# A hybrid decoder block on one core: the q, k, v and attention-gate projections as seven products of halves, later tokens first

## The chip, the core and the metric

The kernel runs on one core of a Trainium2 chip. The core has five engines, each with its own instruction queue that is worked through in order: TensorE (PE, matrix products, which go to PSUM), VectorE (DVE), ScalarE (ACT), GpSimd (POOL) and SyncE (SP), which here only issues DMAs. SBUF is the working memory, 128 partitions wide; PSUM has eight banks of 128 x 512 float32, of which this kernel gives two each to the names `z`, `s`, `o` and `t`. The metric is the device time of one execution in microseconds, the median of several runs.

## What is computed

One decoder layer over 2048 tokens of width 1024, cut to what matters here:

```python
h = rms_norm(x, norm_w) * (1 + scale) + shift          # scale, shift from c
z = h @ w_in                                           # 1024 -> 10240
a, b, g_conv, q, k, v, g_attn, m_conv, m_attn = split(z)
u = silu(layer_norm(causal_conv(a * sigmoid(b)))) * silu(g_conv)
q, k = rope(rms_norm(q, q_norm_w)), rope(rms_norm(k, k_norm_w))   # 12 heads of 128
for group (window, dilation) in ((128, 1), (512, 4), (2048, 16)): # 4 heads each
    o_g, lse_g = dilated_window_attention(q, k, v)
o = sum over groups of softmax(lse) * o_g              # 512 wide
y = sigmoid(m_conv) * (u @ w_conv_out) + sigmoid(m_attn) * ((o * silu(g_attn)) @ w_attn_out)
out = x + gate * (y @ w_out)
```

The attention works on blocks of 128 queries. A block of the group with dilation 16 sees only its own keys; the other groups' blocks also see the block before them of the same residue class, if there is one.

## The kernel before

Every float32 operand of a projection is split into a high part (rounded to the format `float32r` by a ScalarE copy) and a low part (the difference, a subtraction on VectorE or GpSimd, with both of its inputs in SBUF). A product is three matmul terms for each 128 rows of the contraction: high by high, high by low, low by high.

The stages in order:

1. **Start.** The conditioning, the rotary tables (`tab`), the loads of x.
2. **q, k, v.** Twelve heads, one "unit" `u` each, in the order of `GROUPS`; in a unit 16 token blocks `j`. `project_step` runs 24 matmuls (`z_tokens`, L369): the stationary operand is 128 tokens of h, the moving one 384 weight columns (q, k and v of the head). Then it takes sums of squares on ScalarE, a reciprocal root on GpSimd (`rsqrt_cols`, L112 and L113), and the rotary turn on VectorE (L397 to L407), with one SBUF tile as output. During unit 0 the kernel also makes h itself (`h_part`) and writes it to memory (`h_d`).
3. **Attention beside it.** For the first eight units (dilations 4 and 16) q, k, v go to memory (`qkv_d`, L760) and are gathered again by stride (`strided`). The last four units are attended from SBUF. `attend_step` is four parts (`turn_qk`, `scores`, `turn_p`, `values`), one part per block step, entered between the matmuls by `hooks`. `values` writes one DMA per block (L469): 128 output columns with the two softmax numbers behind them.
4. **Gate and merge.** For each of two halves of the 512 gate columns, 16 blocks of 24 matmuls of 256 columns (`merge_z`, `pzg`); `merge_step` weighs the three groups' outputs, multiplies by the gate and writes the result transposed to `ai_d`.
5. **The other columns of w_in** (a, b, g_conv, m_conv, m_attn). They are already done as seven products of halves: tokens and contraction are halved, `column_steps` forms the weight combinations T1 to T4 on GpSimd and splits them, `quad` runs the seven products (L954), the token combinations S1 to S4 lie in `s_d`. The convolution runs on VectorE beside it (`conv_parts`, L1003 to L1043).
6. **Three output projections.**

TensorE's order is the program's own from `pe_order` on (`manual_schedule`). The other engines' order is made by a planner from a timeline that it simulates; inside a queue nothing overtakes. `reuse_waits="tile"` on a pool means that a new tile waits for the last use of the tile whose place it takes.

The lines the argument touches: `z_tokens` (L362), `project_step` (L378), `attend_step` (L419), `merge_load` to `merge_step` (L474 to L528), `unit_weights` (L533), the loop over units (L724), the merge loop (L843), and `column_steps` and `quad` (L896, L944) as the pattern of the new code.

Of the kernel before, what the change touches and what calls it, by code (L numbers as in the profile page):

```python
# [18 lines left out]
P = 128  # L19
# [3 lines left out]
NB = S // P  # L23
TAPS = 31
# [11 lines left out]
GROUPS = (1, 2, 0)  # L36
# [18 lines left out]
def tile_hybrid_block(  # L55
# [22 lines left out]
    qkv_d = {u: dram.tile([S, 3, P], F32, name=f"qkv{u}_d") for u in range(2 * NH)}  # L78
    acc_d = [dram.tile([S, NG, ACC_W], F32, name=f"acc{h}_d") for h in range(NH)]
# [10 lines left out]
    s_d = dram.tile([2, 4, 4, P, 512], F32, name="s_d")  # L90

    t_d = {}
# [22 lines left out]
    tabs_c = pool("tabs")  # L115
    tabs = tabs_c.__enter__()

    tab = tabs.tile([P, NB, 2, 64], F32, tag="tab", name="tab0")
    with pool("start", side="right") as st:
        keep = tc.keep_in_program_order  # L120
# [90 lines left out]
        keep(nc.vector.tensor_scalar(a, a, -2.0, 1.0, op0=ALU.mult, op1=ALU.add))  # L211
        last_mm = {k: ada_row(k) for k in (0, 2, 4, None, 6, 7)}
# [10 lines left out]
    hpool_c = [tc.tile_pool(name=f"hT{i}", bufs=1, side="right", reuse_waits="tile") for i in range(2)]  # L223
    hpools = [c.__enter__() for c in hpool_c]

    def quarter_tile(kh, t, hl, name, dtype=F32R):

        return hpools[0 if t == 0 or (kh, t) == (0, 2) else 1].tile([P, 4, 512], dtype, tag=f"h{hl}{kh}{t}", name=name)

    hi, lo = ({(kh, t): quarter_tile(kh, t, hl, f"hT_{hl}_{kh}{t}") for kh in range(2) for t in range(4)} for hl in ("hi", "lo"))  # L230

    def part(x, k, t0, w, nk=1):

        q = x[k // 4, t0 // 512]
        ks = k % 4 if nk == 1 else slice(k % 4, k % 4 + nk)
        return q[:, ks, t0 % 512 : t0 % 512 + w]


    wpool_c = tc.tile_pool(name="wp0", bufs=8, side="right", reuse_waits="tile")
    wp = wpool_c.__enter__()  # L240
    xpool_c = tc.tile_pool(name="xp", bufs=6, side="right", reuse_waits="tile")
    xp = xpool_c.__enter__()
    hx = {}

    def load_x(j, eng=nc.sync):

        xt = xp.tile([P, D], F32, tag="x", name=f"x{j}")
        i0 = eng.dma_start(xt, x2[P * j : P * j + P, :])
        if j >= 4:
            tc.keep_in_program_order(i0)  # L250
        junk = xp.tile([P, 512], BF16, tag="xn", name=f"xn{j}", bufs=1)
        st = xp.tile([P, 4], F32, tag="st", name=f"xst{j}")
        hx[j] = xt
        halves = [slice(0, 512), slice(512, 1024)]

        def square(i):
            ins = nc.scalar.activation(junk, xt[:, halves[i]], AF.Square, scale=1.0 / 32.0,
                                       accum_out=st[:, i : i + 1])
            if i == 1:
                nc.gpsimd.tensor_add(st[:, 0:1], st[:, 0:1], st[:, 1:2])  # L260
                rsqrt_cols(st[:, 1:2], st[:, 0:1], 1, st[:, 2:3])
            return ins

        def scale(i):
            return nc.scalar.activation(xt[:, halves[i]], xt[:, halves[i]], AF.Copy, scale=st[:, 1:2])

        return [lambda: square(0), lambda: square(1), lambda: scale(0), lambda: scale(1)]

    def h_turn(j, kk, tag="t"):

        pt = bank(tag, f"pt_x{j}_{kk}")
        for a in range(2):
            k = 2 * kk + a
            for b in range(2):
                nc.tensor.transpose(pt[:, 256 * a + P * b : 256 * a + P * b + P], hx[j + b][:, P * k : P * k + P], ident)
        return pt

    def h_first(kk, pt):
        for a in range(2):
            k = 2 * kk + a  # L280
            last = nc.scalar.activation(part(hi, k, 0, 256), pt[:, 256 * a : 256 * a + 256], AF.Identity,
                                 scale=mod[:, KC + k : KC + k + 1], bias=mod[:, k : k + 1])
        for a in range(2):
            k = 2 * kk + a
            hf = xp.tile([P, 2, 256], F32, tag="hf", name=f"hf0_{k}", bufs=2)
            nc.vector.tensor_scalar(hf[:, 0], pt[:, 256 * a : 256 * a + 256], mod[:, KC + k : KC + k + 1],
                                    mod[:, k : k + 1], op0=ALU.mult, op1=ALU.add)
            (nc.gpsimd if a else nc.vector).tensor_tensor(part(lo, k, 0, 256), hf[:, 0], part(hi, k, 0, 256).bitcast(F32),  # L288
                                                          op=ALU.subtract)
            nc.sync.dma_start(h_d[k, :, :256], hf[:, 0])  # L290
        return last

    def h_part(j, kk):
        pt = h_turn(j, kk)
        hf = xp.tile([P, 2, 256], F32, tag="hf", name=f"hf{j}_{kk}", bufs=2)
        for a in range(2):
            k = 2 * kk + a
            nc.vector.tensor_scalar(hf[:, a], pt[:, 256 * a : 256 * a + 256], mod[:, KC + k : KC + k + 1],
                                    mod[:, k : k + 1], op0=ALU.mult, op1=ALU.add)
# [1150 lines left out]
```

## Time and profile before

| | |
|---|---|
| three runs | 2433.52, 2436.54, 2439.67 us (median 2436.54) |
| profiled execution | span 2433.6 us from the first to the last instruction; the page gives no other time of it |
| mean granted TensorE clock | 0.994 |
| stages by the trace | q, k, v and attention from about 45 to 1108 us, gate and merge to 1203 |
| DMA | 372.99 MB, mean 153 GB/s |

The profile's page gives the busy time of each engine (PE matmuls, PEld weight loads), then busy shares in 40 slices, the DMA queues, the chain of work that ended last, and the costliest groups of instructions. In a group's line stand source line, engine, operation, output and inputs by tile names, shapes, count, then busy time and mean duration, then the idle time before the group and what ended it. Durations of pipelined instructions overlap, so the distance between two starts is the price of one. Answers about one source line give the shortest, median and longest duration in ns.

### The profile page before, as it was taken

Reading aid. Unit: us, or ns where it says so; the run is one execution under the profiler, and the core shown is the slowest. Engines: PE = TensorE matmul, PEld = TensorE weight load, DVE = VectorE, ACT = ScalarE, POOL = GpSimd, SP = SyncE. Lnnn points to the kernel's source line nnn. Section 1 sums busy time; section 2 is a strip of 40 time slices with the busy share of each in tenths; the row PEclk is TensorE's granted clock in tenths of the full one; section 3 lists DMA queues with packets and bytes.
Section 4 is the critical chain, followed back from the end, with each engine's and each line's share of the span. In section 5 each row is a group of like instructions: output and inputs, shape, how many; then the busy total and the mean of one; then the engine's idle time right before and its main releaser. Section 6 shows DMA issues by size and latency. Waiting matters only on the chain.

```text
span 2433.6 us, 39444 instructions
## 1 busy us (share of the span) xinstructions
PE 2395.2 (98%) x12881; PEld 2138.5 (88%) x12881; DVE 1688.0 (69%) x3891; ACT 975.0 (40%) x2738; POOL 766.9 (32%) x899
## 2 busy tenths in 40 slices
PE   7999999999999999999999999999999999999999
PEld 3989999999999999999888888878888888888887
DVE  5855655555555565557779999989999968864333
ACT  5733333433344344345544444554444444331000
POOL 4421111111111111112467777765655620000000
PEclk8999999999999999999999999999999999999999
DMA  7633543444452222116663544664444479866443
GB/s 260 219 111 109 160 126 100 147 145 144 147 151 85 68 71 58 32 47 197 200 197 129 161 156 160 208 204 128 141 143 143 152 251 321 274 197 214 126 147 100
DMA packets 342219, 372.99 MB, mean 153 GB/s; under 512 B 29752, under 2 KB 243032, under 8 KB 342014
## 3 DMA queue, kind: packets, MB, share of 16 engines
q1 hardware_dynamic: 328718, 346.80, 45.9%
q10 hardware_dynamic: 13296, 23.66, 2.7%
q8 instruction: 103, 1.69, 0.3%
q14 instruction: 102, 0.84, 0.1%
HBM read 231.74 MB, written 138.61 MB: 152 GB/s over the span
## 4 chain that ended last, share of the span: by engine, by line
PE 92%; DVE 1%; ACT 1%; POOL 1%; DMA 1%; issue 0%; SPq 0%; POOLq 0%; DVEq 0%; ACTq 0%
PE pz L369 31%; PE yc L1230 7%; PE out L1230 7%; PE paab L954 7%; PE ya L1230 4%; PE pag_g_d L954 4%; PE pcab L954 4%; PE pag_mc_d L954 4%; PE pag_ma_d L954 3%; PE ps L441 3%; PE po L460 3%; PE pzg L369 3%; PE pbab L954 2%; PE pcg_mc_d L954 2%; PE pcg_g_d L954 2%; PE ptq L431 2%
## 5 line engine op out<-in xcount | busy, mean ns | idle before, releaser
L369 PE MATMUL pz<-wh_u,hT_lo 128*128 128x384 f32 x1536 | 537.6, 350 | 4.4 <-DVE hT_lo L288 2.5
L369 PE MATMUL pz<-wh_u,hT_hi 128*128 128x384 f32 x1536 | 519.5, 338 | 4.5 <-ACT wh_u L345 2.0
L369 PE MATMUL pz<-wl_u,hT_hi 128*128 128x384 f32 x1536 | 520.5, 339 | 0.4 <-DVE wl_u L348 0.4
L397 DVE SCALAR_TENSOR_TENSOR qk<-pz,st,wqk 128x128 f32<-128x128 f32 x384 | 117.0, 347 | 320.5 <-POOL st L113 320.4
L112 POOL TENSOR_SCALAR st<-st 128x2 f32<-128x2 f32 x192 | 47.7, 248 | 813.9 <-ACT sq L386 813.9
L369 PEld LDWEIGHTS pz<-wh_u,hT_hi 128*128 128x128 f32 x1536 | 291.5, 190 | 7.2 <-ACT wh_u L345 2.9
L369 PEld LDWEIGHTS pz<-wh_u,hT_lo 128*128 128x128 f32 x1536 | 290.0, 189 | 7.4 <-DVE hT_lo L288 3.2
L369 PEld LDWEIGHTS pz<-wl_u,hT_hi 128*128 128x128 f32 x1536 | 290.7, 189 | 1.9 <-DVE wl_u L348 1.4
L433 ACT ACTIVATE qkT<-ptq 128x256 f32<-128x256 f32 x192 | 73.9, 385 | 419.9 <-PE ptq L431 419.4
L1032 DVE SCALAR_TENSOR_TENSOR ce<-us,pair_taps,ce 128x512 f32<-128x512 f32 x240 | 180.3, 751 | 1.7
L1003 DVE SCALAR_TENSOR_TENSOR ce<-ut,chan,ce 128x512 f32<-128x512 f32 x240 | 180.1, 751 | 0.0
L1016 DVE SCALAR_TENSOR_TENSOR cq<-ut,chan,cq 128x512 f32<-128x512 f32 x208 | 156.6, 753 | 4.2
L918 POOL TENSOR_TENSOR slT<-wT,shT 128x512 fp32r<-128x512 f32 x97 | 128.7, 1328 | 75.7 <-ACT shT L917 74.6
L386 ACT ACTIVATE sq<-pz 128x128 bf16<-128x128 f32 x384 | 106.2, 276 | 100.3 <-PE pz L369 93.4
L113 POOL TENSOR_TENSOR st<-st,mhalf 128x2 f32<-128x2 f32 x192 | 136.5, 711 | 16.0
L917 ACT ACTIVATE shB<-wB 128x512 fp32r<-128x512 f32 x120 | 75.5, 630 | 150.4 <-issue 44.5
L917 ACT ACTIVATE shT<-wT 128x512 fp32r<-128x512 f32 x100 | 63.1, 631 | 153.1 <-issue 64.6
L918 POOL TENSOR_TENSOR slB<-wB,shB 128x512 fp32r<-128x512 f32 x77 | 102.0, 1324 | 68.0 <-ACT shB L917 66.4
L446 ACT ACTIVATE sm<-sm,osb 128x128 f32<-128x128 f32 (+1 forms) x192 | 88.8, 463 | 62.6 <-DVE osb L444 59.5
L1413 DVE TENSOR_TENSOR ot<-out,gate_row 128x512 f32<-128x512 f32 x32 | 22.1, 692 | 116.2 <-PE out L1230 116.2
L460 PE MATMUL po<-lv,pT 128*128 128x128 f32 x600 | 97.2, 273 | 0.0
L460 PEld LDWEIGHTS po<-lv,pT 128*128 128x128 f32 x600 | 93.0, 189 | 0.5 <-issue 0.5
(624 smaller groups left out, 6288.7 us busy)
## 6 DMA issues: line engine op xcount, KB each, us to landing
wB<-in_w_in_dram SPq DMA_DIRECT2D x140, 256.0 KB, 3.8
qkv_d<-qkv SPq DMA_DIRECT2D x128, 192.0 KB, 2.2
wT<-tT_d SPq DMA_DIRECT2D x80, 256.0 KB, 2.8
raw_u<-in_w_in_dram SPq DMA_DIRECT2D x93, 192.0 KB, 3.3
lqk<-qkv_d SPq DMA_DIRECT2D x128, 128.0 KB, 2.3
tT_d<-wB ACTq DMA_DIRECT2D x60, 256.0 KB, 2.3
acc_d<-osb SPq DMA_DIRECT2D x192, 65.0 KB, 1.6
at<-acc_d SPq DMA_DIRECT2D x64, 195.0 KB, 3.5
```

The source lines that it names most:

```text
L113: nc.gpsimd.tensor_tensor(dst, scratch[:, :n], mhalf[:, :n], op=ALU.pow)
L369: nc.tensor.matmul(pz[:, :width], part(a, k, P * j, P), w[:, :width], start=(m == 0), stop=(m == 23))
L386: nc.scalar.activation(sq, pz[:, P * i : P * i + P], AF.Square, scale=1.0 / math.sqrt(P), accum_out=st[:, i : i + 1])
L397: nc.vector.scalar_tensor_tensor(qk[:, 2 * i : 2 * i + 2].rearrange("p a b -> p (a b)"), pz[:, P * i : P * i + P], st[:, 2 + i : 3 + i], w ...
L460: nc.tensor.matmul(po[:, :P], box["pT"][:, P * i : P * i + P], vt, start=(i == 0), stop=(i == nk - 1))
L917: nc.scalar.activation(h, q[name], AF.Copy)
L918: eng.tensor_tensor(l, q[name], h.bitcast(F32), op=ALU.subtract)
L954: nc.tensor.matmul(ps, w, x, start=(m == 0 and ps.name not in first), stop=(m == 11 and not more), skip_group_check=True)
L1003: stt(box["e"], e[:, 1 + j : 513 + j], chan[:, cb, 2 * j : 2 * j + 1], box["e"], op0=ALU.mult, op1=ALU.add)
L1016: stt(box["o"], o[:, 2 + j : 514 + j], w, psum_o, op0=ALU.mult, op1=ALU.add)
L1032: stt(dst, box["both"][:, 1 + j : 513 + j], pair_taps[:, cb, j : j + 1], box["e"], op0=ALU.mult, op1=ALU.subtract if j == 0 else ALU.add)
L1230: nc.tensor.matmul(pz, w, xx, start=(m == 0), stop=(m == len(terms) - 1))
```

## The change

The q, k, v and gate columns are now done as the other columns of w_in were: tokens (1024 rows at a time) and contraction (1024) are halved, and two heads make a pair of column halves. Seven products of 512 tokens x 512 rows x 384 columns replace eight. Tokens 1024 to 2047 ("half 1") come first, then tokens 0 to 1023 ("half 0").

- **Start of half 1.** Only x of the later half is made into h before products begin. The gate of the later half is a plain projection, eight blocks of 24 matmuls of 512 columns (`ga_tokens`), written to `ga_d`. The rotary tables go to memory (`tab_d`) and come back; GpSimd multiplies them by the q and k norm weights for each half (`table_weigh`). The combinations S1 to S4 are formed in these eight blocks. h of the earlier half is made during half 1.
- **Product steps.** A pair of heads has 7 products of 4 token blocks, 28 steps of 12 matmuls:

```diff
+        pz = bank("z", f"pz{n}")[:, :w]
+        ah, al = quarters[PRODUCTS[ORDER[pos]][0]]
+        wh, wl = split_of[half, m, pos]
+        terms = [(a, b, k) for k in range(4) for a, b in ((ah, wh), (ah, wl), (al, wh))]
+        for q, (a, b, k) in enumerate(terms):
+            for f in hooks.get(q, ()):
+                f()
+            nc.tensor.matmul(pz, a[:, k, P * i : P * i + P], b[:, k], start=(q == 0), stop=(q == 11))
...
+        if pos == 0:
+            s1 = sums_of["s", i] = tile_of("s1", 4)
+            nc.scalar.activation(s1, pz, AF.Copy)
+            return
+        s1 = sums_of["s", i]
+        if pos == 1:
+            c = tile_of("c", 2)
+            add(c, s1, pz)
+            done(0, 0, c)
+        elif pos == 2:
+            add(s1, s1, pz)
+        elif pos == 3:
+            u3 = sums_of["u", i] = tile_of("u3", 4)
+            add(u3, s1, pz)
+        elif pos == 4:
+            s5 = tile_of("s5", 1)
+            nc.scalar.activation(s5, pz, AF.Copy)
+            c = tile_of("c", 2)
+            add(c, sums_of["u", i], pz)
+            nc.gpsimd.tensor_add(s1, s1, s5)
+            done(1, 1, c)
+        elif pos == 5:
+            add(s1, s1, pz)
+            done(1, 0, s1)
+        else:
+            u3 = sums_of["u", i]
+            add(u3, u3, pz)
+            done(0, 1, u3)
```

`add` is VectorE's addition with one input in PSUM. So each step empties PSUM once, and four of seven products end in `finish`, for 16 finished blocks per pair:

```diff
+    def finish(u, j, c):
...
+        for i in range(2):
+            nc.scalar.activation(sq, c[:, P * i : P * i + P], AF.Square, scale=1.0 / math.sqrt(P),
+                                 accum_out=st[:, i : i + 1])
+        rsqrt_cols(st[:, 2:4], st[:, 0:2], 2, st[:, 4:6])
+        t1 = wk.tile([P, 2, 2, 64], F32, tag="t1", name=f"t1{n}", bufs=4)
+        t3 = wk.tile([P, 2, 2, 64], F32, tag="t3", name=f"t3{n}", bufs=1)
...
+        nc.vector.tensor_tensor(t3.rearrange(flat), c[:, :256], w[:, 1].rearrange("p q c -> p (q c)"), op=ALU.mult)
+        nc.vector.tensor_tensor(t1.rearrange(flat), c[:, :256], w[:, 0].rearrange("p q c -> p (q c)"), op=ALU.mult)
+        nc.vector.tensor_sub(t1[:, :, 0, :], t1[:, :, 0, :], t3[:, :, 1, :])
+        nc.vector.tensor_add(t1[:, :, 1, :], t1[:, :, 1, :], t3[:, :, 0, :])
+        for i in range(2):
+            nc.scalar.activation(t1[:, i], t1[:, i], AF.Copy, scale=st[:, 2 + i : 3 + i])
+        rows = slice(P * j, P * j + P)
+        nc.sync.dma_start(qkv_d[u][rows, 2], c[:, 256:384])
+        nc.sync.dma_start(qkv_d[u][rows, :2], t1.rearrange("p a b c -> p a (b c)"))
```

- **Weights.** In half 1 four raw tiles of 128 x 1536 are loaded for each pair (`raw_load`), GpSimd forms T1 to T4 from them (`raw_make`) and ScalarE's queue stores them to `t_d`. Each product's weights are split in two pieces of 128 x 768 while the product before it runs: in half 1 three of the seven low parts on VectorE, four on GpSimd, in half 0 all on GpSimd, from pieces loaded again:

```diff
+    def raw_make(m, name):
...
+        nc.gpsimd.tensor_tensor(dst, x0, x1, op=ALU.subtract)
+        t_store(name, heads[m], dst, 0)
...
+        split_piece((1, m, pos), name, kp, first_raw[m, name][:, 2 * kp : 2 * kp + 2], W,
+                    nc.vector if pos in (1, 3, 5) else nc.gpsimd)
...
+    def split_again(m, pos, kp):
+        split_piece((0, m, pos), None, kp, next_raw.pop((m, pos, kp)), width_of(JOBS[0][m]), nc.gpsimd)
```

- **Side work of half 1**, by steps: h of the earlier half (`x_again`, `h_part`), its S1 to S4 (`sums_fetch`, `sums_make`), the gate's T1 to T4 (`ga_t_make`), the convolution's channel numbers, the output gate's sum, and loading and splitting the token quarters of half 0 (`land_at`).
- **Attention.** All blocks go through memory and run in half 0, whose seventh job is the gate of the earlier half (28 steps of 12 matmuls of 256 columns). `tick` runs 8/7 times a step. Dilation 1 starts with the later half's blocks, which need four "primer" blocks that only turn the keys. Output and softmax numbers are now two stores:

```diff
+    def tick():
+        if loaded:
+            if loaded[0][0] <= 0:
+                _, u, j, state, primer, got = loaded.pop(0)
+                main.enter(attend(u, j, got, state, primer))
+        for item in loaded:
+            item[0] -= 1
+        if to_attend:
+            u, j, state, primer = to_attend.pop(0)
+            loaded.append([1, u, j, state, primer, block_load(u, j, primer)])
+        for f in main.turn():
+            f()
...
+            nc.sync.dma_start(block_rows(u, acc_d[h])(j)[..., g, :], o[:, :P])
+            nc.sync.dma_start(block_rows(u, lse_d[h])(j)[..., g, :], o[:, P:])
```

- **Merge.** Sixteen items of two blocks and two heads each, entered one in three turns as soon as their blocks are attended (`merge_parts`, `merge_turn`): loads, weights, two joins, transposes. One turn a step in half 0, two a step in the first six products of the next stage, the rest at its seventh:

```diff
+        for _ in range(2 if at < 6 else 0):
+            merge_turn()
+        if at == 6:
+            while merging():
+                merge_turn()
+            close_merge()
```

An item holds four of the five `wide` tiles of 128 x 512 (pool `xs`) and then a fifth for its result. In the stage behind, `wr` has 8 tiles instead of 10, with T2 in two of its own (`wt`), and the scratch tiles are a pool of their own (`spare`).

More of the change, by code (lines that the diff above doesn't have):

```diff
@@ L230, in tile_hybrid_block @@
[L230 to L241, printed above, removed]
@@ L269, in h_turn @@
[L269 to L291, printed above, removed]
```

1144 lines of the change are left out of this document (615 added, 529 removed).

## The prediction

> **What bounds the kernel now.** I read the page's sums first, then the chain of waits, then the busy time of every engine stage by stage.
>
> ```profile
> span 2433.6 us, 39444 instructions
> PE 2395.2 (98%) x12881; PEld 2138.5 (88%) x12881; DVE 1688.0 (69%) x3891; ACT 975.0 (40%) x2738; POOL 766.9 (32%) x899
> PE 92%; DVE 1%; ACT 1%; POOL 1%; DMA 1%; issue 0%; SPq 0%; POOLq 0%; DVEq 0%; ACTq 0%
> ...
> 200.00:400.00 200.00, 200.00 (x1290) 198.75 (x1289) 116.18 (x410) 76.68 (x314) 34.29 (x74) 1.00 0.42 128
> ...
> 1400.00:1600.00 200.00, 196.49 (x860) 162.24 (x860) 191.69 (x278) 97.02 (x172) 149.97 (x117) 0.99 0.58 186
> ```
>
> TensorE is the bound everywhere: 200 of 200 us in the q/k/v stage (columns: length, PE, PEld, DVE, ACT, POOL, clock, DMA share, GB/s). There POOL works only 34 of 200 us. In the stage of the existing products of halves it works 150 of 200. That difference decides this case.
>
> The three terms of a q/k/v product and one of the gate's:
>
> ```profile
> L369 PE MATMUL pz<-wh_u,hT_lo 128*128 128x384 f32 x1536 | 537.6, 350 | 4.4 <-DVE hT_lo L288 2.5
> L369 PE MATMUL pz<-wh_u,hT_hi 128*128 128x384 f32 x1536 | 519.5, 338 | 4.5 <-ACT wh_u L345 2.0
> L369 PE MATMUL pz<-wl_u,hT_hi 128*128 128x384 f32 x1536 | 520.5, 339 | 0.4 <-DVE wl_u L348 0.4
> ...
> L369 PE MATMUL pzg<-wh_ga,hT_hi 128*128 128x256 f32 x256 | 75.7, 296 | 0.0
> ```
>
> Their durations overlap, so I price a matmul by the distance of its starts, from the timeline:
>
> ```profile
> 399.74 0.33 PE L369 MATMUL pz<-wh_u,hT_hi 128*128 128x384 f32 x1
> ...
> 401.82 0.33 PE L369 MATMUL pz<-wh_u,hT_hi 128*128 128x384 f32 x1
> ...
> 1150.60 0.28 PE L369 MATMUL pzg<-wh_ga,hT_hi 128*128 128x256 f32 x1
> ...
> 1152.99 0.28 PE L369 MATMUL pzg<-wh_ga,hT_lo 128*128 128x256 f32 x1
> ...
> 1299.86 0.39 PE L954 MATMUL paab<-hT_hi,shB 128*128 128x512 f32 x1
> ...
> 1305.98 0.39 PE L954 MATMUL paab<-S_hi,shT 128*128 128x512 f32 x1
> ...
> 402.17 0.61 PE L460 MATMUL po<-lv,pT 128*128 128x128 f32 x4
> 402.61 0.38 PE L452 MATMUL ptp<-ident,sm 128*128 128x128 f32 x2
> ```
>
> Twelve steps in 2.08 us are 0.1733 us at 384 columns, twenty in 2.39 are 0.1195 at 256, 27 in 6.12 are 0.2267 at 512.
>
> **Removed on TensorE.** Seven products for eight: 4608 matmuls of 384 columns become 2 x 6 pairs of heads x 28 steps x 12 = 4032; 576 fewer at 0.1733 are -99.8 us. The gate has 3 x 256 of 256 columns (91.8 us) now; then 8 blocks x 24 of 512 (43.5) and 28 x 12 of 256 (40.2), so -8.1. Four primer blocks add 8 transposes, +0.9 at the 0.11 at which four `po` matmuls start below. Attention's other matmuls, the x and merge transposes stay in number. Together **-107 us**, if nothing else becomes late.
>
> **Later half: the new load beside 59.7 us.** A pair of heads is 28 steps x 12 x 0.1733 = 58.2 us on TensorE, some 59.7 with its share of h transposes. A step is 2.08 us instead of 4.16 plus attention, and in it PSUM must be emptied, since `pz` has two banks. Rows for the others' prices:
>
> ```profile
> 400.88 0.22 POOL L112 TENSOR_SCALAR st<-st 128x2 f32<-128x2 f32 x1 [4.26 <-ACT sq L386]
> 401.18 0.71 POOL L113 TENSOR_TENSOR st<-st,mhalf 128x2 f32<-128x2 f32 x1
> ...
> L348 POOL TENSOR_TENSOR wl_u<-raw_u,wh_u x8: 985/996/1977, 5.8 to 43.3; 128x384 fp32r<-128x384 f32 x8
> ...
> 1302.70 1.30 POOL L912 TENSOR_TENSOR wB<-wB,wB 128x512 f32<-128x512 f32 x1 [3.17 <-DVE slB L918]
> ...
> 1306.47 1.29 POOL L912 TENSOR_TENSOR wB<-wB,wB 128x512 f32<-128x512 f32 x1
> ...
> 402.56 0.43 DVE L404 TENSOR_TENSOR t<-qk,tab 128x256 f32<-128x256 f32 x1
> 402.90 0.42 DVE L405 TENSOR_TENSOR qkv<-qk,tab 128x256 f32<-128x256 f32 x1
> ...
> 403.77 0.28 DVE L406 TENSOR_TENSOR qkv<-qkv,t 128x128 f32<-128x128 f32 x1
> 403.97 0.29 DVE L407 TENSOR_TENSOR qkv<-qkv,t 128x128 f32<-128x128 f32 x1
> ```
>
> POOL takes 1.01 us per root (400.88 to 401.89), 0.985 at 384 columns, 1.26 at 512 (three steps in 3.77); so 1.9 at 768 and 3.8 at 1536, scaled by width. Per pair: 16 roots 16.2, eight weight splits of 768 15.2, four raw differences of 1536 15.2, four sums of 384 3.9; with side work (gate differences, tables, two splits, h roots, 29 us in the stage) 55 us of 59.7.
>
> DVE, by starts, takes 0.34 at 256 and 0.20 at 128, about 0.5 at 384. Per pair: 24 PSUM sums 12; 16 finishes of 2 x 0.34 + 2 x 0.20, 17.3; six splits of 768 at 0.95 (between the 0.69 at 512 and the 1.22 at 1024 below), 5.7; side work of 45 us in the stage (h scaling, sums of quarters, gate sums) 7.5. That is 42.5 of 59.7.
>
> Apart, both fit. The next rows say that they don't run apart:
>
> ```profile
> L918 DVE TENSOR_TENSOR slB<-wB,shB x43: 676/689/1769, 1203.7 to 1561.3; 128x512 fp32r<-128x512 f32 x43
> ...
> L839 DVE TENSOR_TENSOR S_lo<-landingS,S_hi x12: 685/1126/1762, 1570.7 to 1597.6; 128x512 fp32r<-128x512 f32 x12
> ...
> L1404 DVE TENSOR_TENSOR yl<-yw,yh x16: 1217/1218/1220, 2209.7 to 2408.2; 128x1024 fp32r<-128x1024 f32 x16
> ...
> L1003 DVE SCALAR_TENSOR_TENSOR ce<-ut,chan,ce x240: 740/751/759, 1245.5 to 1924.2; 128x512 f32<-128x512 f32 x120
> ...
> 1295.64 1.29 POOL L978 TENSOR_TENSOR spare_hi<-spare_hi 128x512 f32<-128x512 f32 x1 [0.73 <-ACT spare_hi L960]
> 1295.73 1.75 DVE L918 TENSOR_TENSOR slB<-wB,shB 128x512 fp32r<-128x512 f32 x1
> ```
>
> A DVE split with both inputs in SBUF takes 0.69 us alone, but 1.75 where a POOL operation had begun 0.09 us earlier: it waited until 1296.93, POOL's end. L1003, one input in SBUF and one in PSUM, never waits (740 to 759 ns over 240). All four operations of `finish` and all splits are of the first kind. So a DVE operation pays for what is left of POOL's, and DVE's queue, with the PSUM sums in it, stands still meanwhile.
>
> The Trainium skill states this too: "SBUF — State Buffer", section "SBUF: two separate sides", calls the pair of ports that the two engines share an exclusive lock, kept for the whole instruction against DVE operations with two SBUF inputs. The trace agrees (1.75 against 0.69 us).
>
> Bounds for the later half. Below: the shared port packed without a gap, 34.3 (POOL's wide operations) + 23.0 (DVE's finishes and splits) + 7.7 of side work = 65 per pair, +5 x 6 = **+31 us**. Above: each wide POOL operation stops DVE for its whole length, 42.5 + 37 = 80, **+120 us**. I take the row nearest: the landing splits lose 1126 - 685 = 0.44 us each where POOL is busy 75%; some 74 such operations per pair (64 + 6 + 4 of side work) lose 32.6, DVE comes to 75 and exceeds TensorE's 59.7 by 15.5: **+93 us**. ACT stays below (16 finishes of two squares and two scalings, 14 splits): it is not charged.
>
> **Earlier half.**
>
> ```profile
> 45.00:1108.00 1063.00, 1053.48 (x6719) 1041.27 (x6719) 626.45 (x2204) 445.45 (x1759) 203.93 (x427) 0.99 0.38 113
> ```
>
> Of these 1053 us, 4608 x 0.1733 = 799 are q/k/v products; 255 are left for attention, transposes and waits, some 210 of them attention, which now all falls here. TensorE needs 349 + 40 + 210, together 600. POOL's wide work is 30 us of some 90 per pair, DVE has 60, so neither bounds. SyncE's queue nearly does: 192 finish stores, 160 weight loads, 776 DMAs for 196 blocks (two loads, and two stores instead of one, from 192), 100 for merges and 20 others, 1250 in 600 us.
>
> ```profile
> 441.18 0.32 SPq L469 DMA_DIRECT2D acc_d<-osb  x1
> ...
> 443.74 0.42 SPq L688 DMA_DIRECT2D sx<-h_d  x1
> ...
> 1134.25 1.75 SPq L477 DMA_DIRECT2D at<-acc_d  x4
> ...
> PE pta L519 <- POOL sg L514: 4.9, 5, 2.9
> ```
>
> Four merge loads in a row take 0.44 us each, five issues with their waits 0.51 (2.56 us). So 550 to 640 us. Queued behind a store that waits are the loads of the next blocks, and TensorE's order, written by hand, waits for those two ticks later. Bounds: 0, if SyncE keeps up; +75, if a third of the 224 ticks wait 1 us, as `pta` did five times. I take 0.5 us an issue, 625 less 600, and a little: **+30**.
>
> **Turn-overs.**
>
> ```profile
> GB/s 260 219 111 109 160 126 100 147 145 144 147 151 85 68 71 58 32 47 197 200 197 129 161 156 160 208 204 128 141 143 143 152 251 321 274 197 214 126 147 100
> ```
>
> The gate blocks of the later half now carry x (2 MB), h out (4), quarters in and sums out (8), gate results (2) and first weights (3): 19 MB in 55 us, where the busiest early slice, at 260 GB/s, would move 14; the first T2 passes POOL in 15 us of the 16.6 before it is due. Bounds 0 to 25, taken **+12**. By the count of turns six merges end among the next stage's first seven products, each over five tiles of which it holds four: 0 to 25, taken **+12**; nothing hides them, because TensorE's order has their transposes there.
>
> **The clock**, uncharged:
>
> ```profile
> 140.00:160.00 20.00, 17.56 (x82) 16.02 (x82) 8.90 (x26) 5.91 (x25) 3.81 (x8) 0.83 0.34 107
> ```
>
> With 2.4 us idle in 20, clock 0.83 means 6.8 us at half rate, 3.4 us lost. Where TensorE waits for DVE anyway, this costs nothing. The skill's "TensorE: Matmul & The Clock Gate", "Part 1: The HAM clock gate (the "warmup" mystery)", wants a wholly idle window of about 3.4 us first; by that, short waits cost nothing, and by the row one in eight does. Twenty such drops would be +68.
>
> **Sum**: 2433.6 - 107 + 93 + 30 + 12 + 12 = 2473.6. The page gives only the span; the three runs' median, 2436.54, is 2.9 above it: **2476.5 us**, slower by 40.
>
> **Rivals.**
> 1. Only TensorE counts: the planner spreads the stalls, as it did at 1400 to 1600, where DVE works 192 of 200 and TensorE 196. For it: that row. Against it: there most of DVE's work is L1003's kind and due late. 2433.6 - 107 + 15 + 2.9 = **2345**, faster.
> 2. The port binds, but packed: +31 there, +5 on SyncE, +24 for the turn-overs: **2390**, faster. It decides below 26 us of port waits a pair: DVE then stands at 68.5, 8.8 over TensorE, and 6 x 8.8 = 53 is what 107 - 30 - 24 leaves. For it: POOL's differences can be done a product early. Against: each engine runs in order, and nothing holds POOL back while DVE is due.
> 3. The ceiling: every wide POOL operation catches DVE, and ticks wait: 2433.6 - 107 + 120 + 75 + 24 + 2.9 = **2549**. For it: differences of 3.8 us, three times the 1.29 shown. Against: the landing row's 0.44 is below half of 1.26.
>
> **How the numbers follow.** Forecast 0.54, by itself 2425 to 2520; rival 1 0.15; rival 2 0.18; rival 3 0.13. Within 0.3% (2429.2 to 2443.9, what a measurement here can tell from no change) lies about 0.06, from the forecast's lower edge; faster 0.15 + 0.18 + 0.02 = 0.35; slower 0.59. The range leaves half of rival 1 and a third of rival 3 out: 2346 to 2540.
>
> **What would show it.** Right: in the later half TensorE below 85% busy, DVE or POOL near 90%; the finish products at 128 x 256 with a median well above 0.42 us; TensorE's longest waits on `pz` from DVE. Then six pairs take about 75 us each instead of 60. SyncE: few gaps in the earlier half, TensorE waiting for `lqk`. Wrong: the finish products at 0.42 us, or TensorE full in both halves (rival 1); matmul starts farther apart than 0.1733 would break the first term.

## The result and the profile after

| | before | after |
|---|---|---|
| median of the runs | 2436.27 us (2433.52 to 2439.67, 4 runs) | 2663.65 us (2656.18 to 2668.63, 4 runs) |
| ratio after to before | | 1.0924, 95% interval 1.0902 to 1.0947 |
| span of the profiled execution | 2433.6 us | 2662.6 us |

The change is slower by 227 us; 2476.5 was predicted. From the page of the kernel after: the span, each engine's busy time, and TensorE's row of tenths over 40 slices.

```profile
span 2662.6 us, 40079 instructions
...
PE 2368.6 (89%) x12073; PEld 2064.0 (78%) x12073; DVE 1923.9 (72%) x3739; ACT 1194.4 (45%) x3092; POOL 1227.5 (46%) x1193
...
PE   5766877888898889989886999999999999999999
```

TensorE has 808 instructions fewer, yet the span is longer. The row of tenths shows where it stands idle: slices 1 to 22, up to 1464 us; behind that it is nearly full, as before. (The page's chain of waits, with 44% for TensorE instead of 92%, can't be compared: followed back from the end, it stops at 1446 us here and says nothing of the stages before.) The busy time by stage (length, then busy us of PE, PEld, DVE, ACT and POOL, granted clock, share of the DMA engines, GB/s), first before, then after:

```profile
45.00:1204.00 1159.00, 1143.31 (x7445) 1129.32 (x7446) 702.52 (x2463) 499.72 (x1927) 235.05 (x464) 0.99 0.40 122
```

```profile
45.00:62.00 17.00, 3.38 (x14) 2.67 (x15) 0.00 (x0) 8.26 (x20) 4.57 (x10) 0.57 0.83 304
62.00:127.00 65.00, 53.58 (x244) 43.01 (x242) 40.93 (x65) 32.92 (x65) 24.27 (x41) 0.90 0.51 168
127.00:145.00 18.00, 0.20 (x1) 0.20 (x1) 5.76 (x6) 3.47 (x6) 3.03 (x3) 0.56 0.92 273
145.00:673.00 528.00, 410.56 (x2094) 387.46 (x2095) 399.18 (x659) 253.53 (x776) 340.11 (x325) 0.90 0.53 171
673.00:1392.00 719.00, 641.12 (x4284) 617.43 (x4282) 472.50 (x1500) 411.99 (x1400) 322.35 (x371) 0.98 0.63 171
1392.00:1460.00 68.00, 39.15 (x145) 28.89 (x145) 39.98 (x101) 34.69 (x69) 30.10 (x39) 0.80 0.87 264
```

These stages against what TensorE alone needs in them by the prediction's distances of starts:

| stage | TensorE alone | predicted | measured | above TensorE |
|---|---|---|---|---|
| until the first gate product | 45 | 45 | 62 | 17 |
| gate blocks, until the first product of halves | 49 | 61 | 82 | 33 |
| later half (145 to 673) | 358 | 451 | 528 | 170 |
| earlier half (673 to 1392) and the 11 us behind | 600 | 630 | 730 | 130 |
| the rest, 1230 us before | 1230 | 1242 | 1260 | 30 |

The last column adds up to 380. The kernel before lost 45 of that too (of its 1159 us, 107 were saved and TensorE alone needs 1007), and 380 - 45 - 107 is the 228 by which the span grew (229.0). With the same 45 the predicted column adds up to the 2473.6 of the prediction's sum.

What TensorE waited for in the later half of the kernel after (total us, times, longest; a wait of 17.8 us that ends at its start belongs to the stage before):

```profile
PE pt_x L320 <- ACT x L300: 34.1, 6, 10.4
PE pz L596 <- DVE u L635: 33.2, 15, 4.0
...
PE pz L596 <- DVE c L616: 12.9, 8, 3.9
```

With seven smaller groups this is 116 us. The other 53 are the clock: 0.90 over 528 us means half rate in a fifth of them, 106 us, and half of that lost. 116 + 53 is the whole 170. The waits for DVE (69 us) were foreseen; the 34 for the scaled x were not. The finish products on DVE between 145 and 620 us (count, busy us, mean ns), which the kernel before did in 425 and 285 ns:

```profile
L567 DVE TENSOR_TENSOR t<-t,t 128x128 f32<-128x128 f32 x82 | 50.1, 611 | 1.5
...
L566 DVE TENSOR_TENSOR t<-c,tw 128x256 f32<-128x256 f32 x43 | 28.5, 665 | 2.7 <-DMA qkv_d<-t 2.5
L565 DVE TENSOR_TENSOR t<-u,tw 128x256 f32<-128x256 f32 x20 | 25.8, 1288 | 8.3 <-ACT xn L293 7.9
```

These three groups take 1.6 to 3 times as long; all the 128x256 products of the half together have a mean of 702 ns. Still DVE is busy 399 of 528 us and POOL 340: neither is full. That is the first sign against a sum that took the later half for as long as its busiest engine.

### The profile page after: what moved, and what is told of

Same layout as the page of the kernel before. It is cut to its first block, busy times and chain, and to the rows that moved or that the text cites. A ratio compares the mean times of both kernels' runs of the same rounds, so it can differ in the third digit from the quotient of the medians.

```text
span 2662.6 us, 40079 instructions
## 1 busy us (share of the span) xinstructions
PE 2368.6 (89%) x12073; PEld 2064.0 (78%) x12073; DVE 1923.9 (72%) x3739; ACT 1194.4 (45%) x3092; POOL 1227.5 (46%) x1193
## 5 line engine op out<-in xcount | busy, mean ns | idle before, releaser
L596 PE MATMUL pz<-sh,S_hi 128*128 128x384 f32 (+1 forms) x832 | 284.4, 342 | 27.0 <-DVE c L627 9.1
L596 PE MATMUL pz<-sl,S_hi 128*128 128x384 f32 (+1 forms) x832 | 294.2, 354 | 0.0
L596 PE MATMUL pz<-sh,A_hi 128*128 128x384 f32 (+1 forms) x624 | 221.3, 355 | 75.5 <-DVE u L635 37.5
L596 PE MATMUL pz<-sh,S_lo 128*128 128x384 f32 (+1 forms) x832 | 281.1, 338 | 0.0
L516 POOL TENSOR_TENSOR sl<-rw,sh 128x768 fp32r<-128x768 f32 (+1 forms) x98 | 174.9, 1791 | 206.9 <-ACT sh L515 173.6
L596 PE MATMUL pz<-sl,A_hi 128*128 128x384 f32 (+1 forms) x624 | 227.1, 364 | 1.2 <-POOL sl L516 1.2
L596 PE MATMUL pz<-sh,A_lo 128*128 128x384 f32 (+1 forms) x624 | 216.8, 347 | 0.0
L596 PEld LDWEIGHTS pz<-sh,S_hi 128*128 128x128 f32 x832 | 160.6, 193 | 36.2 <-DVE s L631 12.1
L596 PEld LDWEIGHTS pz<-sh,S_lo 128*128 128x128 f32 x832 | 161.5, 194 | 0.0
L596 PEld LDWEIGHTS pz<-sl,S_hi 128*128 128x128 f32 x832 | 161.2, 194 | 0.2
```

The source lines that it names most:

```text
L516: eng.tensor_tensor(l, src, h.bitcast(F32), op=ALU.subtract)
L596: nc.tensor.matmul(pz, a[:, k, P * i : P * i + P], b[:, k], start=(q == 0), stop=(q == 11))
```

## The experiments

The times are compared with 2663.65; the profiled execution gives the halves. Each edit was run once, the last one four times; the four runs of the kernel after lie 12.5 us apart, and the kernel before, run again beside the edits, took 2435.6 to 2441.9. An edit lets the planner order every queue but TensorE's anew, so stages that weren't touched moved by up to 11 us; each edit is read in its own stage.

**Finishes through PSUM.** Is it the port?

```diff
-        t3 = wk.tile([P, 2, 2, 64], F32, tag="t3", name=f"t3{n}", bufs=1)
+        if j >= HB:
+            t3 = bank("o", f"t3{n}")[:, :256].rearrange("p (a b c) -> p a b c", a=2, b=2)
+            v = wk.tile([P, W], F32, tag="c", name=f"vc{n}", bufs=2)[:, :P]
+            nc.scalar.activation(v, c[:, 256:384], AF.Copy)
...
+        def c_of(other):
+            return bank("s", f"c{n}")[:, :w] if half else other()
...
-            c = tile_of("c", 2)
+            c = c_of(lambda: tile_of("c", 2))
```

(The fifth and sixth sums go to such a `c` too.)

> In the later half the finished blocks and the first of the two table products lie in PSUM instead of SBUF, and ScalarE copies the v columns to SBUF for the store; so no DVE operation of a finish has two SBUF inputs (the scratch tile that the x squares shared with that table product is theirs alone too). Theory 1, the SBUF port that DVE and POOL share: the table products come down from 640 to 660 ns to near 430, the 128x128 ones from 510 and 411 to near 290, the later half from 528 us to 440 (six pairs of about 73), and with fewer idle gaps its half clock falls too; total about 2570. Rival, the later half is held by the order of the work (x scaling, roots, sums) and not by the port: the durations fall, but the half stays above 500 us and the total above 2635.

2606.64 us, the later half 490. DVE's finish products, and the two halves:

```profile
L571 DVE TENSOR_TENSOR t<-c,tw 128x256 f32<-128x256 f32 x91 | 39.0, 428 | 41.1 <-ACT vc L565 40.4
...
L573 DVE TENSOR_TENSOR t<-t,t 128x128 f32<-128x128 f32 x91 | 25.6, 281 | 0.7
```

```profile
140.00:630.00 490.00, 400.34 (x2095) 380.47 (x2095) 322.00 (x666) 258.07 (x871) 329.41 (x327) 0.91 0.58 186
```

The durations came out as theory 1 says, to 10 ns, with the same POOL work beside them, so the port is shown as their cause. (The Trainium skill, "SBUF — State Buffer", section "SBUF: two separate sides", counts the DVE operations with two SBUF inputs among those that take the lock against POOL; these rows, with one input moved to PSUM, agree.) But the half falls by 38 us where 88 were expected, though DVE works 77 us less. The waits for DVE's sums fall from 69 to 37; those for x stay, at 41. The edit also ends the sharing of one scratch tile with the squares of x, for which DVE had waited 20.5 us in this half, so not all of the 38 need be the port.

**x later.** The squares' scratch gets its own place, and TensorE transposes x four steps later.

```diff
-        junk = wk.tile([P, 512], BF16, tag="t3", name=f"xn{j}", bufs=1)
+        junk = bank("o", f"xn{j}")
...
-            at_step(1, at + 5 + 2 * kk, lambda j=2 * p, kk=kk: h_part(j, kk))
+            at_step(1, at + 9 + 2 * kk, lambda j=2 * p, kk=kk: h_part(j, kk))
```

> The scratch output of the x squares is a PSUM tile of its own instead of the table product's buffer, and the transposes of x stand four steps later in TensorE's order. Theory 2, ScalarE brings the scaled x too late and TensorE, DVE and the next sums queue up behind it: TensorE's 34 us of waits for x go, the 20 us that DVE waits for the scratch go, the later half falls by 35 to 55 us, total 2610 to 2628. Rival (port): TensorE would have waited for DVE anyway; the half falls by less than 15 us, total above 2645.

2653.21 us, the half 516: the rival's side, and theory 2 falls. The trace says why more room didn't help. POOL's timeline of this run (start, us, operation), and TensorE's first transposes of x behind it:

```profile
217.58 0.24 POOL L295 TENSOR_TENSOR xst<-xst 128x1 f32<-128x1 f32 x1
...
219.11 3.42 POOL L531 TENSOR_TENSOR B<-B,B 128x1536 f32<-128x1536 f32 x1
222.61 0.22 POOL L115 TENSOR_SCALAR xst<-xst 128x1 f32<-128x1 f32 x1
...
224.93 3.42 POOL L531 TENSOR_TENSOR T<-B,B 128x1536 f32<-128x1536 f32 x1
228.30 3.41 POOL L531 TENSOR_TENSOR B<-B,B 128x1536 f32<-128x1536 f32 x1
231.68 0.55 POOL L116 TENSOR_TENSOR xst<-xst,mhalf 128x1 f32<-128x1 f32 x1
```

```profile
233.03 0.90 PE L320 MATMUL pt_x<-ident,x 128*128 128x128 f32 x3 [19.49 <-ACT x L300]
```

The root of x takes three small operations, 1.0 us together. In POOL's queue they lie among three differences of raw weights, and the last ends 14.7 us after the first began. ScalarE waits for it, then TensorE, 19.5 us; DVE works only 1.5 and ScalarE 2.2 us of these 14.7, while POOL is full.

**No raw differences.** T1 to T4 are not computed in the later half.

```diff
-            dst = first_raw[m, "T2"] = raws.tile([P, 4, W], F32, tag="t2", name=f"T2_{m}")
+            dst = first_raw[m, "T2"] = first_raw[m, "B22"]
...
-        x0, x1 = first_raw[m, x0], first_raw[m, x1]
-        nc.gpsimd.tensor_tensor(dst, x0, x1, op=ALU.subtract)
```

> POOL's 24 differences of raw weights of 128x1536 in the later half (T1 to T4, 3.6 us each, 86 us) are left out: the tiles are split and stored as they were loaded. DVE's work is the same. Theory 1 (port): DVE's operations with two SBUF inputs lose what these 86 us held them up, the table products come down to about 560 ns, the later half falls by 30 to 50 us, total 2610 to 2635. Rival 1, POOL is late itself (roots and weight splits queued behind the differences): the same fall, but the table products stay above 630 ns. Rival 2, order: less than 15 us.

2606.93 us, the half 476, a little more than either theory gave. The half, and DVE's products in it:

```profile
141.00:617.00 476.00, 394.61 (x2092) 373.32 (x2092) 328.23 (x658) 251.30 (x775) 250.60 (x300) 0.93 0.60 190
```

```profile
L565 DVE TENSOR_TENSOR t<-t,t 128x128 f32<-128x128 f32 x93 | 36.6, 393 | 1.5
L564 DVE TENSOR_TENSOR t<-c,tw 128x256 f32<-128x256 f32 x48 | 35.5, 739 | 0.1
```

The 128x128 products fall from 611 to 393 ns and DVE's busy time by 71 us, which is the port; those from `c` don't fall (665 before), and all 128x256 products together have a mean of 625 ns instead of 702, where theory 1 said 560 and its first rival above 630. So the differences act by the port at least, and the next runs ask whether also by POOL's queue. **Differences in pieces:**

```diff
-        nc.gpsimd.tensor_tensor(dst, x0, x1, op=ALU.subtract)
+        for k in parts:
+            nc.gpsimd.tensor_tensor(dst[:, k], x0[:, k], x1[:, k], op=ALU.subtract)
```

> Each of POOL's 128x1536 differences is cut into four of 128x384 and spread over steps from the end of the pair before to the fourth product, instead of one whole difference at a step; the same elements are worked on. Theory 4, the roots of the finishes and of x stand in POOL's queue behind whole differences (an x root was cut in two by 7 us of them), ScalarE waits for the roots and TensorE for ScalarE: a root now waits 1 us instead of 3.5 to 7, TensorE's waits for x fall from 34 to below 15 us, the later half from 528 to about 495, total about 2630. Rival (port only): DVE is held up by as many elements as before, the half stays within 12 us of 528, total above 2650.

2652.72 us, the half 524, 39.0 us of waits for x. The numbers are the rival's, and what theory 4 expected of smaller pieces fails: TensorE waits for x as long as before (34.1 us). With the finishes through PSUM it is the same:

> The finishes through PSUM and the cut differences together. If port and POOL's queue are two causes, their gains add: the later half from 528 to about 455, total about 2572. If they were the same stall seen twice, it stays near the 490 us of the finishes through PSUM alone, total about 2605.

2608.57 us, the half 493: no gain on top of the 490. POOL's timeline of this run has the second and third operation of an x root:

```profile
317.90 0.23 POOL L115 TENSOR_SCALAR xst<-xst 128x1 f32<-128x1 f32 x1
...
325.03 0.56 POOL L116 TENSOR_TENSOR xst<-xst,mhalf 128x1 f32<-128x1 f32 x1
```

Between them lie five pieces of 1.0 us and two roots of finishes, and the first operation stood at 308.05, seven pieces earlier: 17.5 us from end to end. The planner has put as much work ahead of the root as before, in more pieces.

**The roots and the differences, each left out on top of the finishes through PSUM, then both.** The root's edit:

```diff
-            if i == 1:
+            if i == 1 and root:
                 nc.gpsimd.tensor_add(st[:, 0:1], st[:, 0:1], st[:, 1:2])
                 rsqrt_cols(st[:, 1:2], st[:, 0:1], 1, st[:, 2:3])
...
-            return nc.scalar.activation(hx[j][i], hx[j][i], AF.Copy, scale=st[:, 1:2])
+            return nc.scalar.activation(hx[j][i], hx[j][i], AF.Copy, scale=st[:, 1:2] if root else mod[:, :1])
```

> The finishes through PSUM, and x of the earlier half is scaled by a number that is there already instead of its root mean square: POOL's sum and root of x are left out, the squares stay. Theory 4b, the roots of x in POOL's queue are what makes the scaled x late: against the finishes through PSUM alone (later half 490 us, 41 us of waits for x) the waits fall below 12 us, the half to about 455, total about 2570. Rival, x is late by ScalarE's own queue or by its load: the waits stay above 30 us, total above 2595.

> The finishes through PSUM, and POOL's 24 differences of raw weights in the later half left out. Without the differences alone the total fell by 57 us. Theory 1 (they cost by the port): with DVE's finishes off the port most of that is gone, the later half at 475 to 485 us, total above 2590. Theory 4 (they cost by POOL's queue: roots, weight splits and the sum of the fifth product wait behind them): the gains add, the half falls to about 440, total about 2555.

> The finishes through PSUM, with both the roots of x of the earlier half and POOL's 24 differences of raw weights left out. Alone on top of the finishes they took the later half from 490 to 460 and to 459 us. Two separate stalls: about 430, total about 2553. One stall (x's roots wait in POOL's queue behind the differences) seen twice: 452 to 460, total about 2580.

2584.16, 2584.08 and 2582.41 us. The later half in the three, in this order:

```profile
140.00:601.00 461.00, 396.74 (x2093) 376.46 (x2094) 315.41 (x665) 257.92 (x871) 323.25 (x303) 0.94 0.62 198
```

```profile
143.00:602.00 459.00, 394.97 (x2092) 378.97 (x2093) 286.77 (x666) 258.28 (x872) 244.27 (x304) 0.93 0.63 199
```

```profile
142.00:600.00 458.00, 395.68 (x2093) 378.26 (x2094) 287.83 (x667) 257.56 (x873) 237.02 (x283) 0.93 0.63 200
```

Taking 24 short operations from POOL (three for each x root), or 24 of 3.5 us, or both, comes to the same, and TensorE's waits for x fall from 41 to 14, 15 and 8 us: it is one stall, of some 32 us once the port is off (490 to 458), and its place is the roots of x behind the differences in one queue. POOL's sum of work (323 us against 244) hardly matters.

**Six PSUM banks.** How much comes of TensorE having only one step in hand?

```diff
-        pz = bank("z", f"pz{n}")[:, :w]
+        pz = bank("zso"[(PER * m + 4 * pos + i) % 3] if half else "z", f"pz{n}")[:, :w]
```

> In the later half the products' sums go round six PSUM banks instead of two (the four of the attention's scores and results, which lie idle there); nothing else is changed. Theory 6, TensorE has only one step of 2.1 us in hand, so each burst of late work on DVE or ScalarE (a held port, a root, x) stops it, though DVE's sum over a pair would fit: with five steps in hand the waits for pz fall from 77 to below 25 us, the later half from 528 to about 450, total about 2575. Rival, DVE is late over the whole pair (throughput), or the order behind x decides: the half stays above 505 us, total above 2635.

2646.56 us, the half 501, between the two (the total is on the rival's side). TensorE's waits in the later half:

```profile
PE pt_x L320 <- ACT x L300: 51.2, 6, 22.5
...
PE pz L596 <- DVE sl L516: 18.4, 8, 5.6
PE pt_ch L719 <- DMA ch<-in_conv_ln_b_dram: 18.1, 1, 18.1
PE pz L596 <- POOL sl L516: 10.6, 9, 4.2
```

The waits for DVE's sums are gone (69 to 3 us), though DVE works as much as before (394 us), so they were bursts; but TensorE, now ahead, meets the next late thing: x, split weights, a transfer. The last experiment of this kind puts a finish's block and its product into one bank, so that four are left for the products, with the roots and the differences left out as above:

```diff
+                both = bank("s", f"c{n}")
+                add(both[:, :256], x0[:, :256], pz[:, :256])
+                add(v, x0[:, 256:], pz[:, 256:])
+                finish(job[side], j, both, both[:, 256:].rearrange("p (a b c) -> p a b c", a=2, b=2), v)
```

> As the run before, but a finish's block and table product share one PSUM bank (the v columns are summed straight into SBUF by DVE, ScalarE's copy of them goes), so that the products' sums can go round four banks instead of two. If what is left are short bursts on DVE and ScalarE that one step in hand can't cover, the later half falls to 380 to 400 us, 20 to 40 above its matmuls. If it is a load, it stays within 12 us of the run before.

2557.04 us:

```profile
141.00:572.00 431.00, 380.19 (x2091) 367.76 (x2091) 294.26 (x748) 239.44 (x763) 225.56 (x269) 0.95 0.66 210
```

Against 458 it gains 27 us, less than the 60 to 80 of the bursts theory and more than the 12 of its rival. Of the 73 us above TensorE's 358, 22 are clock (5% of 431) and 51 are waits, the largest for x (17.8) and for DVE's sum of the v columns (15.0). Those 51 were not taken apart further.

**The earlier half: three tiles for q and k, then one store too.**

```diff
-        qk = att.tile([P, 2, P], F32, tag="lqk", name=f"lqk{n}", bufs=2)
+        qk = att.tile([P, 2, P], F32, tag="lqk", name=f"lqk{n}", bufs=3)
...
-            qkT = att.tile([P, 2, P], F32, tag="qkT", name=f"qkT{n}", bufs=4)
+            qkT = att.tile([P, 2, P], F32, tag="qkT", name=f"qkT{n}", bufs=3)
...
-            nc.sync.dma_start(block_rows(u, acc_d[h])(j)[..., g, :], o[:, :P])
-            nc.sync.dma_start(block_rows(u, lse_d[h])(j)[..., g, :], o[:, P:])
+            nc.sync.dma_start(block_rows(u, acc_d[h])(j)[..., g, :], o)
```

> Three tiles instead of two for the loaded q and k of an attention block (one fewer of the transposed ones, for the room). Theory 3, the load of a block can only be issued after the transposes of the block two before, and then has too little time: TensorE's 41 us of waits for it in the earlier half fall below 15, the half from 719 us to about 680, total about 2622. Rival, SyncE's queue itself is too slow or stands at waiting stores: the waits stay above 30 us, total above 2650.

> Three tiles for the loaded q and k, and the attention results stored by one DMA for a block instead of two, as in the kernel before (192 DMAs fewer on SyncE's queue, 32 more for the merges' short loads). Theory 3b, SyncE's queue itself is too slow (161 to 209 DMAs and 67 to 91 us busy per pair): against three tiles alone (2651) another 20 to 30 us less, total about 2625, waits for q and k below 10 us. Rival, the queue stands at stores that wait and its length matters little: less than 8 us, total above 2643.

2650.94 and 2624.57 us; the earlier half 709, then 684. TensorE's waits for q and k in it, first in the kernel after, then with three tiles:

```profile
PE ptq L825 <- DMA lqk<-qkv_d: 40.9, 32, 3.4
PE po L858 <- DVE pT L851: 11.7, 15, 1.6
PE ps L837 <- ACT qkT L827: 8.8, 12, 2.9
```

```profile
PE ptq L825 <- DMA lqk<-qkv_d: 26.3, 25, 3.3
```

With one store they are gone from the list. The tile count gave the half 10 us of the 39 expected, the 160 fewer issues 25 more, as the theory of a queue too slow says. The two stores for a block were the price of this change for SyncE, and they cost more than the tiles.

**The turn-overs.** x of the first two blocks and the last gate results go into tiles of pool `xs`, and the first raw weights are loaded from two queues.

```diff
+        if j < HB + 2:
+            hx[j] = [wide(f"x{j}_{i}") for i in range(2)]
...
-    for name in ("B11", "B12", "B22", "B21"):
-        raw_load(0, name)
+    for name, eng in (("B11", nc.scalar), ("B12", nc.sync), ("B22", nc.scalar), ("B21", nc.sync)):
+        raw_load(0, name, eng)
```

> Only the two turn-overs: x of the first two blocks is loaded into tiles of another pool instead of quarter tiles that lie over the start's memory; the last gate results lie in that pool too, and the first raw weights (B11 first) are issued by ScalarE's and SyncE's queues side by side. Theory 5, both stages begin late because their loads wait for memory of the stage before: the first gate product moves from 62 to about 50 us, the first product of halves from 82 to about 70 us behind it, total about 2640. Rival, the loads are late by bandwidth or by the modulation, not by memory: less than 8 us in all.

2666.5 us. In the kernel after, the first loads of x and of the raw weights (queue, line, count) and the products that wait for them:

```profile
41.90 0.82 ACTq L307 DMA_DIRECT2D x12hi<-in_x_dram  x2
...
136.25 1.12 SPq L500 DMA_DIRECT2D B<-in_w_in_dram  x2
```

```profile
62.39 0.78 PE L381 MATMUL pga<-gah,A_hi 128*128 128x512 f32 x1
...
144.80 0.69 PE L596 MATMUL pz<-sh,A_hi 128*128 128x384 f32 x1 [17.82 <-ACT sh L515]
```

And with the edit, the first raw load and the products, then POOL at the start of the gate blocks:

```profile
122.73 0.39 ACTq L506 DMA_DIRECT2D B<-in_w_in_dram  x1
```

```profile
48.67 0.79 PE L387 MATMUL pga<-gah,A_hi 128*128 128x512 f32 x1 [4.84 <-ACT A_hi L336]
...
72.75 0.90 PE L326 MATMUL pt_x<-ident,x12lo 128*128 128x128 f32 x3 [15.39 <-ACT x12lo L300]
...
134.01 0.69 PE L602 MATMUL pz<-sh,A_hi 128*128 128x384 f32 x1 [11.69 <-ACT sh L521]
```

```profile
57.55 4.32 POOL L419 TENSOR_TENSOR tw<-tab,wqk 128x256 f32<-128x256 f32 x6 [1.62 <-DMA tab<-tab_d]
61.83 0.37 POOL L295 TENSOR_TENSOR xst<-xst 128x1 f32<-128x1 f32 x1
...
71.38 1.09 POOL L116 TENSOR_TENSOR xst<-xst,mhalf 128x1 f32<-128x1 f32 x2
```

The first gate product comes 14 us earlier, so memory held its x back. The first raw load is issued 0.4 us behind the last gate product instead of 9.3, and the wait for the weights falls from 17.8 to 11.7 us: memory again, though here the queues changed too. But between them TensorE waits 15 us for x of the next blocks, and the first product of halves comes 10.8 us earlier, not 24. Those blocks were loaded (from 47 us on) and their squares taken (by 58); it is the root of x again. Its three operations stand in POOL's queue among the products of the rotary tables with the norm weights (`tw`), and the last ends at 72.5. The kernel after has the same wait there, 10.2 us. The later half takes 539 us instead of 528, why was not traced, and the total shows nothing.

**What adds up.** The two halves' edits together, and then with four banks:

> The finishes through PSUM, three tiles for the loaded q and k, and one store for a block's results. The two halves' gains should add, as they lie in different stages: 2663 - 57 - 38 = 2568, between 2560 and 2576. Above 2590 one of them would be given back later.

> Nothing left out: finishes in one PSUM bank each and four banks for the products' sums in the later half, three tiles for the loaded q and k, one store for a block's results. Six banks alone brought the later half to 501 us by taking the waits for DVE away and leaving those for x (51); the finishes through PSUM alone brought it to 490. Bursts and port are separate: later half about 465, earlier half 682, total about 2555. If x's wait takes up what the banks free, the half stays near 490, total about 2580. Either way slower than the kernel before (ratio 1.05 to 1.06).

2579.96 us: the halves are 490 and 682, as each alone, so these gains do add (38 and 37). The total is 12 above the expectation, since the 57 and 39 of the single runs held some 20 us of stages that weren't edited. And 2566.29 us, ratio to the kernel before 1.0534 (95% interval 1.0516 to 1.0551), with nothing left out: later half 466, as expected, with 44 us of waits for x left; earlier 687. No version tried beats the kernel before.

## Why the prediction was too low

**The direction and its cause held.** TensorE lost its place as the bound in the later half (78% busy; below 85 was predicted), the 128x256 finish products rose from 0.42 to 0.70 us on average, and in PSUM they fell back. The 107 us saved are there as far as the count shows: TensorE has 808 instructions fewer (576 and 240 less, 8 more). But DVE or POOL "near 90%" did not come: DVE was busy 76% of the half, POOL 64%.

**"+93" for the later half was 170.** Two steps failed. "DVE comes to 75 and exceeds TensorE's 59.7 by 15.5" took the pair to be as long as its busiest engine. DVE had only 66.5 us of work a pair (399 / 6; of the 0.44 us that I charged to each operation, a finish's lost 0.20: 77 us over 64 x 6), and the pairs took 80 to 99. With one step in hand, lateness on different engines adds instead of hiding: taken away one after the other, the port (with the scratch) gave 38 us, the root chain 32, the two banks 27, and 73 stay even without these, of which 22 are clock and 51 waits whose cause stays open. The ceiling of +120, "each wide POOL operation stops DVE for its whole length", was no ceiling, since it counted one engine alone. The other step is one left out: POOL's roots were counted as load (16.2 us a pair) and never as a wait. The rule that I gave for SyncE, what is queued behind a waiting instruction, I did not ask of POOL's differences.

**"The clock, uncharged" cost 53 us in the later half alone.** The claim "where TensorE waits for DVE anyway this costs nothing" is wrong: the half rate comes after the wait, in the work behind it. Each us of waiting carried 0.46 more (53 / 116), in the run with four banks and both left out 0.43 (22 / 51), in the earlier half, whose waits are 3.4 us at most, 0.18 (14 / 78). The row quoted there, with 3.4 us lost beside 2.4 us idle, had shown that short waits cost, and the "+68" for twenty drops is what the two halves came to (53 and 14); the reason for leaving it out of the sum does not hold.

**"+30" for the earlier half was 130.** SyncE's queue was the right place: TensorE waited 41 us for q and k, and the two edits took 35 us off the half (719 to 684). Not priced were TensorE's other waits in this half, 37 us, the largest for the copies of the attention weights (11.7) and of the turned q and k (8.8), and the clock, 0.98, another 14. TensorE itself was busy for 641 us, 627 without those 14: its own work is some 27 us more than the 600 of the sum, in which the 210 for attention was an estimate. With the 11 us behind the half, in which TensorE waits for the next stage's first weights, this is the whole 130 (41 + 37 + 14 + 27 + 11).

**"+12" and "+12" for the turn-overs were 50 and 30.** The bandwidth argument missed what happened. The loads wait for memory of the stage before: x is issued at 41.9 us, when the start's tiles come free (its wait: 15.2 us), and the raw weights wait for the gate results' tiles (17.8); between them a root of x stands behind the table products on POOL (11.0). The merges are as foreseen in kind, but larger; TensorE's waits between 1392 and 1500 us:

```profile
PE pta L948 <- POOL sg L942: 17.6, 9, 4.9
PE pag_g_d L1120 <- ACT shB L1083: 10.6, 1, 10.6
```

The first are the merges' transposes; with some 10 us of clock (0.83 over the 57 us from 1403 on) they make up the 30. The second is the 11 us counted with the earlier half.

**The rivals.** Rivals 1 and 2 needed DVE to hide its port waits; rival 3, the slowest, came nearest and was still too small, for the reasons above.

## What to carry to other kernels

Busy times per stage give a lower bound only: where engines hand a step on in turn and TensorE has one buffer in hand, add the lateness of each hand-over, not the excess of the busiest engine, and add a part of every wait again for the clock (here 0.18 to 0.46 of it). Look for short operations (a root, a store) that a critical chain needs and that share a queue with long ones; cutting the long ones up doesn't help while the same amount is queued ahead. Shortening the bound engine's steps is worth little when the others' work per step stays.

## What the runs showed of the hardware

The granted clock goes by windows of 3.41 us, and a partly idle window is enough to halve the next. From the busy times of the kernel after, in such windows (length, PE, PEld, DVE, ACT, POOL, clock, DMA share, GB/s):

```profile
412.53:415.94 3.41, 1.25 (x7) 1.25 (x8) 2.16 (x7) 0.81 (x4) 1.05 (x4) 0.99 0.72 218
415.94:419.36 3.42, 3.42 (x13) 3.42 (x12) 3.42 (x4) 0.80 (x4) 3.34 (x1) 0.51 0.83 268
...
477.26:480.68 3.42, 1.61 (x10) 1.29 (x9) 1.50 (x5) 2.31 (x5) 3.42 (x5) 1.00 0.99 295
480.68:484.09 3.41, 3.31 (x11) 2.80 (x9) 2.66 (x3) 1.52 (x6) 3.25 (x4) 0.51 0.66 225
```

TensorE is busy 1.25 us in one window and 1.61 in another, and the window behind each runs at half clock, full of work. In the second there is one wait, of 1.81 us. With this execution cut into such windows from 146 us on, each of the 737 has a clock of 0.50 or 0.51, or of 0.99 or 1.00. 29 windows at full clock were followed by half clock, all idle for 50% or more, and 659 were not, all idle for 54% or less. Out of the half clock, 30 windows were followed by full clock, all idle for 18% or less, and 18 by half clock again, all idle for 16% or more. So a wait of 1.8 us can cost 1.7 more, and further waits in the slow window prolong it. The Trainium skill ("TensorE: Matmul & The Clock Gate", "Part 1: The HAM clock gate (the "warmup" mystery)") gives the same window, but says that an idle one brings the half clock; these rows say that a half idle one does.
